# Rotary scores over 128 rows, SwiGLU blocks turned off TensorE, HGRN2 queries and forget features token-major

## The chip, the core and the metric

The kernel runs on one core of one Trainium2 chip. The metric is the time of one execution on the device in microseconds (us), lower is better. A core has TensorE (PE in the profile: matmuls, with the load of the stationary operand shown apart as PEld), VectorE (DVE), ScalarE (ACT), GpSimd (POOL) and the queue engine SyncE (SP), which issues most transfers here.

## What is computed

One layer on 256 tokens of width 2048, in float32: a half-step SwiGLU feed-forward (width 5632), a mixer of two branches (HGRN2, a gated linear recurrence over chunks of 64 tokens with 16 heads of 128, and latent attention with 16 heads whose scores have a 128-wide plain part and a 64-wide rotary part), a read of a memory of 256 rows, and a second SwiGLU half-step. Cut to what the change touches:

```python
def swiglu_half_step(x, pre_g, w_gate, w_up, w_down, post_g):
    h = rms_norm(x, pre_g)
    y = (jax.nn.silu(h @ w_gate) * (h @ w_up)) @ w_down
    return x + FFN_RESIDUAL_WEIGHT * rms_norm(y, post_g)
...
    q_full = jnp.concatenate([q_nope, q_pe], axis=-1)          # 128 + 64 per head
    k_full = jnp.concatenate(
        [k_nope, jnp.broadcast_to(k_pe[:, :, None, :], (B, S, MLA_HEADS, QK_ROPE))], axis=-1)
    o_b = chunk_causal_attention(q_full, k_full, v, MLA_QK ** -0.5)
...
    q_in = jax.nn.silu(q_hg.astype(f32)).reshape(B, S, HG_HEADS, HG_KDIM)
    o_a = hgrn2_chunk_scan(q_in, k_in, log_f, v_in).astype(x.dtype)   # k_in, log_f from f_hg
```

## The kernel before

Every large product is made of three matmuls: weights and activations are each split into a high part in the fp32r format and the rest (`whi`, `wlo`; `hh`, `hl`), and hi*hi + lo*hi + hi*lo are added up in PSUM. The small products of attention and HGRN2 are plain float32 matmuls, and the trace shows each of those as two records, called passes here. Weights stream from memory in pieces of 128x1024 (a "pair": two blocks of 128 rows by 512 columns), in the order of a list, `plan`. For each piece `feed` issues the transfer of `raw`, an ACT cast to `whi` and a DVE subtraction to `wlo`; there are three buffers for split pieces, so the cast of a piece waits until TensorE has finished with the piece three before it. `gemm` holds activations (128 tokens wide) stationary and streams 512 weight columns: 12 matmuls per pair, a result of two PSUM banks (`m` = 0, 1 for the two halves of the tokens) laid out token-major. `gemm_T` holds weights stationary and streams all 256 tokens: 24 matmuls per pair, and the result is feature-major, which is what the following step needs.

In `ffn`, each of 44 blocks (22 per SwiGLU, in segments of 12 and 10) is one `gemm` named `gu` of 8 pairs; then ACT takes the silu into `sg`, DVE multiplies into `h`, four TensorE transposes bring `h` to `pT` feature-major, and `part_split` makes `fh` (ACT) and `fl` (DVE), the stationary operands of the product `dn` that ends the segment.

In `attend`, a head's scores for the two halves of the queries are each two matmuls into one bank, the plain part over 128 rows and the rotary part over 64 rows (rows 0 to 63 or 64 to 127 by the head's parity, against `kpeT`, which holds the rotated key twice).

In `hgrn_units`, for each of four groups of four heads, the query `hq` and the forget feature `hf` are made by `gemm_T` (feature-major), the output gate `og` and the value `hv` by `gemm`, in the order hq, og, hv, hf. The query and forget features are scaled per token on DVE with `rB`, a broadcast of the norm factors. `hgrn` then runs a long chain of ACT and DVE steps (log, exp, a scan `b`, seven levels of exponentials `e`), with small matmuls `dg`, `lv`, `lx`, `o` between; all that overlaps the large products of the next group. PE, ACT and DVE each run their instructions in the order that the program's scheduler wrote them; an instruction that waits holds up those behind it on its engine.

Of the kernel before, what the change touches and what calls it, by code (L numbers as in the profile page):

```python
# [37 lines left out]
class Layer:  # L38
    def __init__(self, ctx, tc, A):
# [19 lines left out]
        self.q = []  # L59
        self.pending = []  # L60
        self.ident = self.cst.tile([P, P], F32, name="ident")
        make_identity(nc, self.ident)
# [22 lines left out]
    def feed(self, ahead):  # L85
        nc = self.nc
        while self.ready < min(self.at + ahead, len(self.plan)):
            src = self.plan[self.ready]
            spare = self.ready in self.spare
            n = src.shape[-1]  # L90
            raw = self.wraw.tile([P, n], F32, name=self.nm("raw"), tag="raw")
            nc.sync.dma_start(out=raw, in_=src)
            if spare:
                hi, lo = self.slot(self.spare[self.ready], "whi", F32R), self.slot(self.spare[self.ready], "wlo", F32R)
            else:
                hi = self.wsp.tile([P, n], F32R, name=self.nm("whi"), tag="whi")
                lo = self.wsp.tile([P, n], F32R, name=self.nm("wlo"), tag="wlo")
            nc.scalar.activation(hi, raw, AF.Copy)  # L98
            nc.vector.tensor_tensor(lo, raw, hi.bitcast(F32), ALU.subtract)  # L99
            self.q.append((hi, lo))  # L100
            self.ready += 1
# [9 lines left out]
    def gemm(self, act, k0, k1, name="g", head=0, tail=0, warm=0):  # L111
# [6 lines left out]
        for grp in groups:  # L118
            if grp[0] >= head and (grp[0] - head) % 2 == 0:
                self.settle(1)  # L120
            w = [self.weights(self.pending and grp[0] > head) for _ in grp]
            ks = [k0 + 2 * t + c for t in grp for c in range(2)]
            order = [(k, m) for k in ks for m in range(2)] if len(ks) == 2 else [(k, m) for m in range(2) for k in ks]
# [49 lines left out]
    def gain_split(self, hi, lo, pieces):  # L173
# [3 lines left out]
        for o, ps, g in pieces:  # L177
            self.last_lo = nc.vector.scalar_tensor_tensor(lo[:, o], ps, self.gc[:, g : g + 1], hi[:, o].bitcast(F32), ALU.mult, ALU.subtract)  # L178
        return ins

    def block_T(self, hi, lo, x, gcols=None, scale=None):
# [84 lines left out]
    def ffn(self, st, which, aside=None):  # L266
# [4 lines left out]
        for si, (b0, b1) in enumerate(SEG):  # L271
            quads = []
            for b in range(b0, b1):
# [9 lines left out]
                for m in range(2):  # L283
                    sg = self.tmp("sg")
                    nc.scalar.activation(sg[:, :256], ps[m][:, :256], AF.Silu, scale=r[m])
                    nc.vector.scalar_tensor_tensor(h[:, m * 256 : m * 256 + 256], ps[m][:, 256:], r[m], sg[:, :256], ALU.mult, ALU.mult)
                pt = self.bank("pT")
                for c in range(2):
                    for m in range(2):
                        nc.tensor.transpose(pt[:, c * 256 + m * P : c * 256 + m * P + P], h[:, m * 256 + c * P : m * 256 + c * P + P], self.ident)  # L290
                s = slice(512 * ((b - b0) % 2), 512 * ((b - b0) % 2) + 512)
                self.part_split(hi[:, s], lo[:, s], pt)
            fa = self.halves([q[0] for q in quads], [q[1] for q in quads])
# [73 lines left out]
    def mixer_consts(self):  # L367
        nc, v, c = self.nc, self.nc.vector, self.cst
        self.ones = c.tile([P, P], F32, name="ones")
        nc.gpsimd.memset(self.ones, 1.0)  # L370
        self.lmask = c.tile([P, 12 * 64], U8, name="lmask")
# [36 lines left out]
        nc.gpsimd.dma_start(out=fr, in_=self.A["invf"].to_broadcast([P, 32]))  # L408
        ang, n, tail, w = (c.tile([P, 64], F32, name=s) for s in ("ang", "angn", "angt", "angw"))
        for m_ in range(2):  # L410
# [68 lines left out]
    def key_pe(self, act, r):  # L479
# [22 lines left out]
        for m in range(2):  # L502
            nc.tensor.transpose(pt[:, m * P : m * P + P], k2[:, m * P : m * P + P], self.ident)
        self.kpeT = self.cst.tile([P, 256], F32, name="kpeT")
        nc.vector.tensor_copy(self.kpeT, pt[:, :256])

# [24 lines left out]
    def attend(self, g, qn, kn, qpe, value):  # L531
# [3 lines left out]
        for h in range(4):  # L535
            c = 256 * h
            rows = slice(64 * (h % 2), 64 * (h % 2) + 64)
            pc = 256 * ((4 * g + h) // 2 % 4)
            ps = self.bank("sc")
            for m, n0 in ((0, 0), (1, P)):  # L540
                w = P + P * m
                o = ps[:, n0 : n0 + w]
                nc.tensor.matmul(o, lhsT=qn[:, c + m * P : c + m * P + P], rhs=kn[:, c : c + w], start=True, stop=False)
                nc.tensor.matmul(o, lhsT=qpe[rows, pc + m * P : pc + m * P + P], rhs=self.kpeT[rows, :w], start=False, stop=True)
            s = self.tmp("s")
# [32 lines left out]

    def hgrn_units(self, g, act, actT, r, rB):
        nc = self.nc  # L580
        rb2 = rB.rearrange("p (o t) -> p o t", o=1).to_broadcast([P, 2, 256])


        def feature(ps, name, swap):
            o = self.slot("A", name)
            halves = lambda t: t.rearrange("p (h x t) -> p h x t", h=2, x=2)
            for i in range(2):
                ov, pv = halves(o[:, 512 * i : 512 * i + 512]), halves(ps[i])
                if not swap:
                    nc.vector.tensor_tensor(o[:, 512 * i : 512 * i + 512].rearrange("p (h t) -> p h t", h=2), ps[i].rearrange("p (h t) -> p h t", h=2), rb2, ALU.mult)  # L590
                    continue
                for x in range(2):
                    rx = rB[:, P * x : P * x + P].unsqueeze(1).to_broadcast([P, 2, P])
                    nc.vector.tensor_tensor(ov[:, :, 1 - x, :], pv[:, :, x, :], rx, ALU.mult)
            return o

        q = feature(self.gemm_T(actT, KC, "hq"), "q", True)
        nc.scalar.activation(q, q, AF.Silu)
        ps = self.gemm(act, 0, KC, "og")
        og = self.slot("A", "og")  # L600
        for m in range(2):
            nc.scalar.activation(og[:, m * 512 : m * 512 + 512], ps[m], AF.Silu, scale=r[m])
        ps = self.gemm(act, 0, KC, "hv")
        v = self.slot("A", "v")
        for m in range(2):
            nc.scalar.activation(v[:, m * 512 : m * 512 + 512], ps[m], AF.Identity, scale=r[m])
        f = feature(self.gemm_T(actT, KC, "hf"), "f", False)
        return q, f, v, og
# [137 lines left out]
    def mixer(self, st):  # L746
# [6 lines left out]
        for m in range(2):  # L753
            V.tensor_scalar(rh[:, m : m + 1], r[m], 0.5, None, ALU.mult)
        rB = self.cst.tile([P, 256], F32, name="rB")
        ps = self.bank("rB")
        for m in range(2):
            dg = self.tmp("dg")
            V.tensor_scalar(dg[:, :P], self.ident, r[m], None, ALU.mult)
            nc.tensor.matmul(ps[:, m * P : m * P + P], lhsT=self.ones, rhs=dg[:, :P], start=True, stop=True)  # L760
        V.tensor_copy(rB, ps[:, :256])
        qpe = [self.query_pe(self.gemm(self.halves(*cqT), 0, 4, "qr")) for _ in range(2)]
# [16 lines left out]
        for g in range(4):  # L779
            gr = self.hgrn_units(g, act, actT, r, rB)  # L780
            oa.append(self.hgrn(g, *gr))
# [26 lines left out]
    def plan_mixer(self):  # L808
# [7 lines left out]
        for j in range(4):  # L816
            pl += win(22 + j)
        group = lambda g: win(g) + win(12 + g) + win(8 + g) + win(4 + g)
        full = lambda k: [A[k][j, t] for j in range(4) for t in range(KC // 2)]
# [179 lines left out]
```

## Time and profile before

| | |
|---|---|
| median of 3 runs | 2651.07 us (2650.95 to 2651.12) |
| the profiled execution's own time | 2651.14 us |
| its span, first to last instruction | 2649.1 us, mean granted TensorE clock 0.999 |
| PE busy | 2622.8 us, 99% |
| DVE busy | 1497.3 us, 57% |
| ACT busy | 1311.8 us, 50% |
| transferred | 481.39 MB, mean 182 GB/s |

The profiled execution's time is its span and 2.0 us around it; it lies 0.07 us above the median. Busy time of PE counts a matmul from its start to its modelled end, and matmuls overlap: what one costs is read from start to start, not from its length.

### The profile page before, as it was taken

To read this page: it belongs to the slowest core of one execution; us is meant where nothing else is said; L and a number is where in the kernel's file an instruction comes from. 1 tells how busy PE (TensorE), PEld (TensorE's weight loads), DVE (VectorE), ACT (ScalarE), POOL (GpSimd) and SP (SyncE) were. 2 spreads that over 40 slices of the span, in tenths; PEclk is the share of its full clock that TensorE was granted. 3 is DMA by queue.
4 is the path that set the end of the run, shared out by engine and by line. 5 is a ranking of instruction groups with operands and counts; after the bars stand their busy time and mean duration, and the time that the engine had idled before them with its cause. 6 is when DMAs were issued, how large, how long until landed. Compare 5 with 4: busy or idle time off the path is not lost.

```text
span 2649.1 us, 33984 instructions
## 1 busy us (share of the span) xinstructions
PE 2622.8 (99%) x13136; PEld 2215.3 (84%) x13136; DVE 1497.3 (57%) x2004; ACT 1311.8 (50%) x1750; POOL 13.2 (0%) x36
## 2 busy tenths in 40 slices
PE   9999999999999999999999999999999999999998
PEld 7888888888888888889989988889788888888886
DVE  6555444554576544447577575657655554455555
ACT  5444444444455444346666664555644444444443
POOL 0000000000000000000000000000000000000000
PEclk9999999999999999999999999999999999999999
DMA  6655555555654346555545545665455556655564
GB/s 230 191 188 187 190 196 192 188 188 189 202 171 144 111 155 195 191 191 160 167 154 165 168 161 189 205 205 178 149 193 191 188 188 193 195 191 188 189 194 161
DMA packets 133714, 481.39 MB, mean 182 GB/s; under 512 B 15024, under 2 KB 15040, under 8 KB 133552
## 3 DMA queue, kind: packets, MB, share of 16 engines
q1 hardware_dynamic: 131472, 473.49, 55.4%
q0 software_dynamic: 1504, 4.68, 0.6%
q8 instruction: 103, 1.69, 0.3%
q10 hardware_dynamic: 576, 1.05, 0.1%
q14 instruction: 59, 0.48, 0.1%
HBM read 477.06 MB, written 2.10 MB: 181 GB/s over the span
## 4 chain that ended last, share of the span: by engine, by line
PE 96%; DVE 2%; DMA 1%; ACT 1%; issue 0%; SPq 0%; DVEq 0%; ACTq 0%
PE gu L130 12%; PE gu L129 12%; PE gu L128 12%; PE dn L128 6%; PE dn L129 6%; PE dn L130 6%; PE gate L130 2%; PE gate L128 2%; PE gate L129 2%; PE wo L129 1%; PE wo L130 1%; PE wo L128 1%; PE hf L352 1%; PE hf L351 1%; PE hf L350 1%; PE hv L129 1%
## 5 line engine op out<-in xcount | busy, mean ns | idle before, releaser
L99 DVE TENSOR_TENSOR wlo<-raw,whi 128x1024 fp32r<-128x1024 f32 x893 | 1092.5, 1225 | 1045.4 <-ACT whi L98 1044.3
L98 ACT ACTIVATE whi<-raw 128x1024 fp32r<-128x1024 f32 x893 | 945.9, 1060 | 1084.0 <-PE gu L130 444.9
L129 PE MATMUL gu<-wlo,hh 128*128 128x512 f32 x1408 | 552.1, 392 | 1.4 <-DVE wlo L99 1.4
L130 PE MATMUL gu<-whi,hl 128*128 128x512 f32 x1408 | 549.1, 390 | 0.7 <-DVE hl L178 0.7
L128 PE MATMUL gu<-whi,hh 128*128 128x512 f32 x1408 | 496.6, 393 | 1.8 <-ACT whi L98 1.5
L128 PEld LDWEIGHTS gu<-whi,hh 128*128 128x128 f32 x1408 | 263.9, 188 | 60.2 <-ACT whi L98 2.1
L130 PEld LDWEIGHTS gu<-whi,hl 128*128 128x128 f32 x1408 | 264.4, 188 | 55.7 <-DVE hl L178 1.5
L129 PEld LDWEIGHTS gu<-wlo,hh 128*128 128x128 f32 x1408 | 264.5, 188 | 55.0 <-DVE wlo L99 2.2
L129 PE MATMUL dn<-wlo,fh 128*128 128x512 f32 x704 | 274.2, 390 | 0.0
L130 PE MATMUL dn<-whi,fl 128*128 128x512 f32 x704 | 274.0, 389 | 0.0
L128 PE MATMUL dn<-whi,fh 128*128 128x512 f32 x704 | 247.1, 390 | 0.0
L128 PEld LDWEIGHTS dn<-whi,fh 128*128 128x128 f32 x704 | 132.1, 188 | 27.8
L130 PEld LDWEIGHTS dn<-whi,fl 128*128 128x128 f32 x704 | 132.2, 188 | 27.3
L129 PEld LDWEIGHTS dn<-wlo,fh 128*128 128x128 f32 x704 | 132.2, 188 | 27.1
L129 PE MATMUL gate<-wlo,hh 128*128 128x512 f32 x256 | 100.7, 394 | 0.0
L130 PE MATMUL gate<-whi,hl 128*128 128x512 f32 x256 | 100.1, 391 | 0.0
L128 PE MATMUL gate<-whi,hh 128*128 128x512 f32 x256 | 91.8, 391 | 0.0
L351 PE MATMUL hf<-hl,whi 128*128 128x256 f32 x256 | 72.5, 284 | 0.0
L351 PE MATMUL hq<-hl,whi 128*128 128x256 f32 x256 | 72.4, 284 | 0.0
L350 PE MATMUL hf<-hh,whi 128*128 128x256 f32 x256 | 72.3, 283 | 0.0
L350 PE MATMUL hq<-hh,whi 128*128 128x256 f32 x256 | 72.1, 283 | 0.0
L352 PE MATMUL hf<-hh,wlo 128*128 128x256 f32 x256 | 71.8, 283 | 0.0
(358 smaller groups left out, 3544.3 us busy)
## 6 DMA issues: line engine op xcount, KB each, us to landing
raw<-in_ffn_gu_dram SPq DMA_DIRECT2D x352, 512.0 KB, 3.4
raw<-in_win_dram SPq DMA_DIRECT2D x208, 512.0 KB, 3.5
raw<-in_ffn_dn_dram SPq DMA_DIRECT2D x176, 512.0 KB, 3.5
raw<-in_wbb_dram SPq DMA_DIRECT2D x32, 512.0 KB, 3.4
raw<-in_wba_dram SPq DMA_DIRECT2D x32, 512.0 KB, 3.5
raw<-in_wo_dram SPq DMA_DIRECT2D x32, 512.0 KB, 3.6
gb<-in_grow_dram POOLq DMA_DIRECT2D x16, 256.0 KB, 4.6
raw<-in_qup_n_dram SPq DMA_DIRECT2D x8, 512.0 KB, 3.4
```

What stands on the lines that cost most here:

```text
L98: nc.scalar.activation(hi, raw, AF.Copy)
L99: nc.vector.tensor_tensor(lo, raw, hi.bitcast(F32), ALU.subtract)
L128: nc.tensor.matmul(ps[m], lhsT=ah, rhs=wh[:, c], start=(k == k0), stop=False)
L129: nc.tensor.matmul(ps[m], lhsT=ah, rhs=wl[:, c], start=False, stop=False)
L130: self.last_mm = nc.tensor.matmul(ps[m], lhsT=al, rhs=wh[:, c], start=False, stop=(k == k1 - 1))
L350: nc.tensor.matmul(o, lhsT=wh[:, c], rhs=ah, start=first, stop=False)
L351: nc.tensor.matmul(o, lhsT=wh[:, c], rhs=al, start=False, stop=False)
L352: nc.tensor.matmul(o, lhsT=wl[:, c], rhs=ah, start=False, stop=last)
```

## The change

Four edits. (1) `ffn` no longer transposes `h` on TensorE: `turn` has DVE transpose `h` within blocks of 32x32 (`hb`), and 16 ACT copies of 32 partitions by 128 values put the blocks where the full transpose has them (`hT`); `part_split` reads `hT`. These ACT jobs are deferred: four strips to a job and the split as a fifth, one job behind each weight cast from the third pair after the block on. (2) `hq` and `hf` become `gemm` calls, token-major like `og` and `hv`; ACT scales them (with the silu, for the query) into `ta`, DVE transposes the 32x32 blocks into `tb`, and 16 strips for each half of the tokens, alternating between ACT and DVE, put them in place. The order of a group is now hq, og, hf, hv. (3) The rotary part of the scores contracts over all 128 rows, against a key tile `kpeT` that holds zeros in the other head's 64 rows. (4) `rB` and its two matmuls are gone.

```diff
@@ feed, gemm
-            nc.scalar.activation(hi, raw, AF.Copy)
+            self.last_hi = nc.scalar.activation(hi, raw, AF.Copy)
...
             w = [self.weights(self.pending and grp[0] > head) for _ in grp]
+            if self.later and self.later[0][0] <= self.at:
+                with self.tc.issue_after(self.last_hi.ins):
+                    self.later.pop(0)[1]()
@@ new
+    def turn(self, h, hi, lo):
+        nc = self.nc
+        b, o = self.tmp("hb"), self.tmp("hT")
+        nc.vector.transpose(b, h)
+        bv = b.rearrange("p (m c q t) -> p m c q t", m=2, c=2, q=4)
+        ov = o.rearrange("p (c m x t) -> p m c x t", c=2, m=2, x=4)
+        def strips(x):
+            for q in range(4):
+                nc.scalar.activation(ov[32 * q : 32 * q + 32, :, :, x, :], bv[32 * x : 32 * x + 32, :, :, q, :], AF.Copy)
+        self.defer([lambda x=x: strips(x) for x in range(4)] + [lambda: self.part_split(hi, lo, o)])
+    def defer(self, jobs):
+        self.later += [(self.at + 3, f) for f in jobs]
+    def turn_heads(self, ps, r, func, name, swap):
+        nc = self.nc
+        o = self.slot("A", name)
+        ov = o.rearrange("p (c m x t) -> p m c x t", c=4, m=2, x=4)
+        def strips(b, m, half):
+            bv = b.rearrange("p (c q t) -> p c q t", c=4, q=4)
+            for x in (2 * half, 2 * half + 1):
+                for q in range(4):
+                    to, src = ov[32 * q : 32 * q + 32, m, :, x, :], bv[32 * x : 32 * x + 32, :, q, :]
+                    if (x + q) % 2 == 0:
+                        nc.scalar.activation(to, src, AF.Copy)
+                    else:
+                        nc.vector.tensor_copy(to, src)
+        for m in range(2):
+            a, b = self.tmp("ta"), self.tmp("tb")
+            nc.scalar.activation(a, ps[m], func, scale=r[m])
+            nc.vector.transpose(b, a)
+            self.defer([lambda b=b, m=(1 - m if swap else m), x=x: strips(b, m, x) for x in range(2)])
+        return o
@@ ffn
-                pt = self.bank("pT")
-                for c in range(2):
-                    for m in range(2):
-                        nc.tensor.transpose(pt[:, c * 256 + m * P : c * 256 + m * P + P], h[:, m * 256 + c * P : m * 256 + c * P + P], self.ident)
...
-                self.part_split(hi[:, s], lo[:, s], pt)
+                self.turn(h, hi[:, s], lo[:, s])
@@ key_pe
-        self.kpeT = self.cst.tile([P, 256], F32, name="kpeT")
-        nc.vector.tensor_copy(self.kpeT, pt[:, :256])
+        self.kpeT = self.cst.tile([P, 512], F32, name="kpeT")
+        nc.gpsimd.memset(self.kpeT, 0.0)
+        for h in range(2):
+            nc.vector.tensor_copy(self.kpeT[64 * h : 64 * h + 64, 256 * h : 256 * h + 256], pt[64 * h : 64 * h + 64, :256])
@@ attend
-                nc.tensor.matmul(o, lhsT=qpe[rows, pc + m * P : pc + m * P + P], rhs=self.kpeT[rows, :w], start=False, stop=True)
+                nc.tensor.matmul(o, lhsT=qpe[:, pc + m * P : pc + m * P + P], rhs=self.kpeT[:, kc : kc + w], start=False, stop=True)
@@ hgrn_units
-        q = feature(self.gemm_T(actT, KC, "hq"), "q", True)
-        nc.scalar.activation(q, q, AF.Silu)
+        q = self.turn_heads(self.gemm(act, 0, KC, "hq"), r, AF.Silu, "q", True)
...
+        f = self.turn_heads(self.gemm(act, 0, KC, "hf"), r, AF.Identity, "f", False)
         ps = self.gemm(act, 0, KC, "hv")
...
-        f = feature(self.gemm_T(actT, KC, "hf"), "f", False)
```

In the order of ACT's instructions, one block of the first SwiGLU (the second `gu` product ends, the third runs) stood so before; `whi` are the casts of weight pieces:

```order
L98 ACTIVATE whi_680<-raw_678 128x1024
L285 ACTIVATE sg_645<-gu_498,ry_379 128x256
L98 ACTIVATE whi_698<-raw_696 128x1024
L285 ACTIVATE sg_648<-gu_499,ry_393 128x256
L98 ACTIVATE whi_716<-raw_714 128x1024
L98 ACTIVATE whi_734<-raw_732 128x1024
L169 ACTIVATE fh_404<-pT_651 128x512
```

The same stretch of a block on ACT in the changed kernel:

```order
L332 ACTIVATE sg_830<-gu_663,ry_379 128x256
L99 ACTIVATE whi_879<-raw_877 128x1024
L332 ACTIVATE sg_833<-gu_664,ry_393 128x256
L99 ACTIVATE whi_901<-raw_899 128x1024
L197 ACTIVATE hT_837<-hb_836 32x2x2x32 x8
L99 ACTIVATE whi_923<-raw_921 128x1024
L197 ACTIVATE hT_837<-hb_836 32x2x2x32 x4
L99 ACTIVATE whi_945<-raw_943 128x1024
L197 ACTIVATE hT_837<-hb_836 32x2x2x32 x4
L99 ACTIVATE whi_967<-raw_965 128x1024
L173 ACTIVATE fh_827<-hT_837 128x512
```

The split moves from behind four casts to behind six, and sixteen strips stand between the casts, eight of them in one run.

In the HGRN2 stage, on ACT around the end of a group's recurrence (`sx` is the copy of the small product `lx`, `sq` sums squares of the output `o`), the order before was:

```order
L98 ACTIVATE whi_10154<-raw_10152 128x1024
L715 ACTIVATE sx_9579<-lx_9581 128x512
L201 ACTIVATE sq_9594,sso_9589<-o_9587 128x128
L201 ACTIVATE sq_9596,sso_9589<-o_9587 128x128
L201 ACTIVATE sq_9598,sso_9589<-o_9587 128x128
L98 ACTIVATE whi_10172<-raw_10170 128x1024
```

In the changed kernel the query of the next group is taken out of PSUM there, with a load of an activation table ahead of it, and `whi_10234` is the cast of the fourth weight piece of `hf` (the tiles of pieces one to three are cast ahead of these rows):

```order
L99 ACTIVATE whi_10216<-raw_10214 128x1024
L743 ACTIVATE sx_9756<-lx_9758 128x512
L223 ACT_TABLE_LOAD
L223 ACTIVATE ta_9987<-hq_9840,ry_6139 128x512
...
L223 ACTIVATE ta_9991<-hq_9841,ry_6153 128x512
...
L217 ACTIVATE q_9986<-tb_9988 32x4x32 x5
L630 ACTIVATE og_10173<-og_9995,ry_6139 128x512
L630 ACTIVATE og_10173<-og_9996,ry_6153 128x512
L217 ACTIVATE q_9986<-tb_9992 32x4x32 x4
...
L99 ACTIVATE whi_10234<-raw_10232 128x1024
```

Between two casts there were four short instructions; now there are two `ta`, two `og`, sixteen strips, five `sq` and a table load.

On PE, the `hf` product of the same group began so before, with both result banks (10209, 10210) in turn and 24 matmuls to a weight piece:

```order
L350 MATMUL hf_10209<-hh_5556,whi_10213 128x256
L351 MATMUL hf_10209<-hl_5560,whi_10213 128x256
L350 MATMUL hf_10210<-hh_5556,whi_10213 128x256
L351 MATMUL hf_10210<-hl_5560,whi_10213 128x256
L352 MATMUL hf_10209<-hh_5556,wlo_10214 128x256
```

It begins so in the changed kernel, 15 matmuls to the one bank (10176) from three pieces (10180, 10198, 10216), and then 15 to the other (10177) from the same pieces:

```order
L752 MATMUL o_9765<-v_9601,sx_9756 128x128
L132 MATMUL hf_10176<-whi_10180,hh_5859 128x512
L133 MATMUL hf_10176<-wlo_10181,hh_5859 128x512
L134 MATMUL hf_10176<-whi_10180,hl_5863 128x512
...
L132 MATMUL hf_10176<-whi_10216,hh_5860 128x512
L133 MATMUL hf_10176<-wlo_10217,hh_5860 128x512
L134 MATMUL hf_10176<-whi_10216,hl_5864 128x512
L132 MATMUL hf_10177<-whi_10180,hh_5859 128x512
```

The bank 10177 is the one that `hq` held; the first piece is used up after 21 matmuls of 512 columns. The run of DVE's recurrence between two splits (a scan, two masked products, one product, four steps on f) is the same in both kernels; the split behind it belonged to the first piece of the next group's `og` before, and belongs to the fifth piece of its `hq` now.

## Rows read from the trace of the kernel before

**Rows 1.** The page, busy us by engine (share of the span), instructions.

```profile
PE 2622.8 (99%) x13136; PEld 2215.3 (84%) x13136; DVE 1497.3 (57%) x2004; ACT 1311.8 (50%) x1750; POOL 13.2 (0%) x36
```

**Rows 2.** The page, the chain that ended last, shares of the span by engine.

```profile
PE 96%; DVE 2%; DMA 1%; ACT 1%; issue 0%; SPq 0%; DVEq 0%; ACTq 0%
```

**Rows 3.** Windows: from:to length, busy (instructions) of PE PEld DVE ACT POOL, PEclk, DMA.

```profile
414.02:636.32 222.30, 222.30 (x998) 183.31 (x996) 112.21 (x107) 98.90 (x110) 0.00 (x0) 1.00 0.59 189
636.32:745.66 109.34, 109.34 (x485) 90.44 (x484) 61.99 (x69) 48.87 (x57) 1.61 (x3) 1.00 0.67 208
1024.39:1111.43 87.04, 87.04 (x385) 72.10 (x384) 43.01 (x39) 34.73 (x34) 0.00 (x0) 1.00 0.59 194
1111.43:1134.46 23.03, 23.03 (x193) 23.02 (x192) 11.28 (x12) 8.47 (x8) 0.00 (x0) 1.00 0.58 184
1134.46:1156.25 21.79, 21.79 (x98) 18.03 (x97) 10.77 (x11) 11.20 (x11) 0.00 (x0) 1.00 0.60 192
1201.04:1305.11 104.07, 103.04 (x694) 94.91 (x693) 73.45 (x114) 68.62 (x100) 0.00 (x0) 1.00 0.52 162
```

**Rows 4.** Timeline of PE, three transposes inside a gu product: start us, length us.

```profile
67.05 0.39 PE L128 MATMUL gu<-whi,hh 128*128 128x512 f32 x1
67.28 0.49 PE L290 MATMUL pT<-ident,h 128*128 128x128 f32 x3
...
67.84 0.40 PE L130 MATMUL gu<-whi,hl 128*128 128x512 f32 x1
68.08 0.40 PE L128 MATMUL gu<-whi,hh 128*128 128x512 f32 x1
```

**Rows 5.** Timeline of PE, scores of one group of four heads, first to last.

```profile
894.98 0.38 PE L543 MATMUL sc<-cp,cp 128*128 128x128 f32 x2
...
897.38 0.49 PE L544 MATMUL sc<-kpeT,qpeT 64*128 64x128 f32 x2
...
903.23 0.50 PE L128 MATMUL vv<-whi,ch 128*128 128x512 f32 x1
```

**Rows 6.** Tile sc, line 868 (memory read's scores, 128 rows): first and last start.

```profile
L868 PE MATMUL sc<-cp,cp x16: 377/379/379, 1848.8 to 1852.1; 128*128 128x256 f32 x16
```

**Rows 7.** The chain in order of time: start, us, piece; 128-column float32 passes.

```profile
1239.62 1.78 PE lv L684 x16
```

**Rows 8.** Groups of ACT by form, with mean ns of one behind the busy us.

```profile
L98 ACT ACTIVATE whi<-raw 128x1024 fp32r<-128x1024 f32 x893 | 945.9, 1060 | 1084.0 <-PE gu L130 444.9 <-PE dn L130 232.5 <-PE gate L130 56.7
L201 ACT ACTIVATE sq<-o 128x128 bf16<-128x128 f32 x32 | 8.8, 277 | 7.9 <-PE o L724 6.1 <-PE o L722 1.2
L732 ACT ACTIVATE on<-o,ry 128x128 f32<-128x128 f32 x32 | 8.6, 382 | 0.0
L201 ACT ACTIVATION_READ_ACCUMULATOR sq<-o 128x1 f32 x32 | 6.3, 195 | 0.0
L598 ACT ACT_TABLE_LOAD x4 | 5.1, 1283 | 0.1
L606 ACT ACTIVATE v<-hv,ry 128x512 f32<-128x512 f32 x8 | 5.8, 728 | 1.0 <-PE hv L130 1.0
```

**Rows 9.** Timeline of ACT: eight 128x128 activations back to back, start and length.

```profile
1279.66 2.16 ACT L732 ACTIVATE on<-o,ry 128x128 f32<-128x128 f32 x8
```

**Rows 10.** Groups of DVE by form, mean ns of one.

```profile
L99 DVE TENSOR_TENSOR wlo<-raw,whi 128x1024 fp32r<-128x1024 f32 x893 | 1092.5, 1225 | 1045.4 <-ACT whi L98 1044.3
L527 DVE COPY cp<-kn 128x512 f32<-128x512 f32 x8 | 5.5, 691 | 1.3 <-PE kn L352 1.2
L153 DVE SCALAR_TENSOR_TENSOR ry<-rt,ry 128x1 f32<-128x1 f32 x48 | 7.4, 157 | 0.8
```

**Rows 11.** Waits in 1201 to 1513 us: us in total, times, longest.

```profile
PE og L129 <- DVE wlo L99: 3.1, 3, 1.0
```

**Rows 12.** Timeline of DVE in one group: two wlo splits, first and last.

```profile
1218.40 1.23 DVE L99 TENSOR_TENSOR wlo<-raw,whi 128x1024 fp32r<-128x1024 f32 x1 [0.97 <-ACT whi L98]
...
1225.25 1.22 DVE L99 TENSOR_TENSOR wlo<-raw,whi 128x1024 fp32r<-128x1024 f32 x1
```

More of the change, by code (lines that the diff above doesn't have):

```diff
@@ L60, in __init__ @@
         self.pending = []
+        self.later = []
         self.ident = self.cst.tile([P, P], F32, name="ident")
@@ L368, in mixer_consts @@
         nc, v, c = self.nc, self.nc.vector, self.cst
-        self.ones = c.tile([P, P], F32, name="ones")
-        nc.gpsimd.memset(self.ones, 1.0)
         self.lmask = c.tile([P, 12 * 64], U8, name="lmask")
@@ L408, in mixer_consts @@
         nc.gpsimd.dma_start(out=fr, in_=self.A["invf"].to_broadcast([P, 32]))
-        ang, n, tail, w = (c.tile([P, 64], F32, name=s) for s in ("ang", "angn", "angt", "angw"))
+        wk = self.tmp("ang")
+        ang, n, tail, w = (wk[:, 64 * i : 64 * i + 64] for i in range(4))
         for m_ in range(2):
@@ L536, in attend @@
             c = 256 * h
-            rows = slice(64 * (h % 2), 64 * (h % 2) + 64)
+            kc = 256 * (h % 2)
             pc = 256 * ((4 * g + h) // 2 % 4)
@@ L576, in attend, with hgrn_units @@
         return hi, lo
-    def hgrn_units(self, g, act, actT, r, rB):
+    def hgrn_units(self, g, act, r):
         nc = self.nc
[L581 to L595, printed above, removed]
-        q = feature(self.gemm_T(actT, KC, "hq"), "q", True)
-        nc.scalar.activation(q, q, AF.Silu)
+        q = self.turn_heads(self.gemm(act, 0, KC, "hq"), r, AF.Silu, "q", True)
         ps = self.gemm(act, 0, KC, "og")
@@ L754, in mixer @@
             V.tensor_scalar(rh[:, m : m + 1], r[m], 0.5, None, ALU.mult)
[L755 to L761, printed above, removed]
         qpe = [self.query_pe(self.gemm(self.halves(*cqT), 0, 4, "qr")) for _ in range(2)]
@@ L779, in mixer @@
         for g in range(4):
-            gr = self.hgrn_units(g, act, actT, r, rB)
+            gr = self.hgrn_units(g, act, r)
             oa.append(self.hgrn(g, *gr))
@@ L817, in plan_mixer @@
             pl += win(22 + j)
-        group = lambda g: win(g) + win(12 + g) + win(8 + g) + win(4 + g)
+        group = lambda g: win(g) + win(12 + g) + win(4 + g) + win(8 + g)
         full = lambda k: [A[k][j, t] for j in range(4) for t in range(KC // 2)]
```

## The prediction

> **What bounds the kernel now.** The page comes first: TensorE is busy for 99% of the span, DVE for 57% and ACT for 50% [rows 1], and the chain of work that ended last lies on PE for 96% of the span [rows 2]. So a matmul taken away shortens the kernel by its own step, as long as DVE and ACT still deliver weights in time; work put on DVE or ACT costs nothing until a cast or a split of weights comes late. The windows give the prices by stage. Ten gu products of 96 matmuls fill 222.30 us, four bb products of the same 96 matmuls, with nothing between them, 87.04 us, which is 21.76 us a product and 0.2267 us a matmul of 512 columns; an hq product, 192 matmuls of 256 columns, takes 23.03 us, an og product right behind it 21.79 us [rows 3]. The granted clock is 1.00 in all of them, the 2.4 GHz level. In the gu window ACT is busy for 98.90 us and DVE for 112.21 us of 222.30 us [rows 3], so both have room there. One HGRN2 group takes 104.07 us, with DVE busy for 73.45 us [rows 3]; this is where PE waits.
>
> **SwiGLU transposes.** 44 blocks lose 4 transposes each, 176 in all. In the timeline three of them stand between two gu matmuls: from 67.05 to 68.08 us is 1.03 us, where three steps of 0.2267 us would take 0.68 us, so one costs 0.117 us and 176 cost 20.5 us [rows 4]. The windows give more: 222.30 - 10 x 21.76 = 4.7 us, and the dn window, which holds the transposes of the last block, is 109.34 us against 480 x 0.2267 = 108.8 us; together 5.2 us for ten blocks, 0.52 us a block, 23 us in all [rows 3]. I take 22 us, and keep 20.5 and 23.
>
> What replaces them must stay hidden. DVE gets one 32x32-block transpose of 128x512 a block. The trace has none; the nearest row of that size is a copy of 128x512 at 0.69 us [rows 10], and a two-times slower one would still fit, as DVE works 112.21/10.2 = 11 us a block of 21.8 us. ACT gets 16 strips of 32x128. The nearest rows are 128x128 activations: 0.277 us alone from PSUM and 0.382 us alone with a per-row scale [rows 8], and eight back to back in 2.16 us, so (2.16 - 0.38)/7 = 0.25 us a step [rows 9]. I take 0.25 us, with 0.38 us as the upper bound (the same instruction with nothing overlapped) and 0.16 us as the lower (the shortest instruction of a neighbouring engine [rows 10]). A block's ACT time goes from 98.90/10.2 = 9.7 us to 13.7 us (15.8 us at the upper bound), of 21.8 us. The tightest place is the run of eight strips between two casts: a cast may start when the piece three before is used up, and its split is wanted two pieces later, 2 x 2.72 = 5.44 us; cast and split take 1.06 + 1.23 us [rows 8, 10], so 3.1 us are free. Eight strips push the next cast back by 1.06 + 2.0 - 2.72 = 0.3 us (1.4 us at the upper bound). That is inside, so I price this edit's cover at nothing; it would begin to show at about 0.6 us a strip. The split `fh` of a segment's last block comes some five pieces into dn, which wants it in piece 10 or 12.
>
> **hq and hf token-major.** 192 steps of 256 columns become 96 of 512: 23.03 us become 21.77 us, for eight products 8 x 1.26 = 10.1 us [rows 3].
>
> **Scores.** A group of four heads takes 903.23 - 894.98 = 8.25 us, 2.06 us a head, where every second pair of passes is 64 rows high [rows 5]. The same float32 passes, all 128 rows high, step by 3.3/15 = 0.22 us at 256 columns [rows 6] and 1.78/16 = 0.11 us at 128 columns [rows 7]; a head has four of each, 1.31 us. So the passes on either side of a change of height cost about 0.1 us more than their columns. With none left, 0.75 us a head is saved, 12 us for 16. In the first two groups other matmuls stand between the passes and some of the changes are missing already, so I take 10.5 us, and keep 9 and 12. The softmax behind the scores then gets its input faster than DVE works it off; I allow 0.5 us of new waits.
>
> **rB.** Two float32 matmuls, four passes of 0.11 us [rows 7]: 0.4 us.
>
> **The HGRN2 stage.** Before: 2 x 23.03 + 2 x 21.79 us of products and 116 passes of 0.11 us (dg, lv, lx, o and transposes) make 102.5 us of the 104.07 us [rows 3, 7], so 1.5 us a group is waiting, in three groups; 1.0 us of it is og waiting for a split [rows 11] that stood behind DVE's long run: 5.6 us between two splits [rows 12]. After, by the changed order, three places a group can wait:
>
> First, hf's first 15 matmuls all go to one bank, because the other still holds hq until ACT has taken `ta`. So the first three pieces come free late, the first after 21 matmuls (4.8 us) and not 12. ACT's row behind `sx` is: table load 1.28, two `ta` of 512 columns, like the 0.73 us of a scaled hv bank, two `og` at the same, sixteen strips at 0.25 and five sums of squares at 0.28 and 0.2 us for their read-out [rows 8]; with some 0.6 us for `sx` that makes 1.3 + 1.5 + 1.4 + 4.0 + 2.3 + 0.6 = 11 us before the cast of piece four. From the end of `lx` PE has 2.7 us of small passes and 36 matmuls, 8.2 us: it wants that piece at 10.9 us. Cast and split end at some 12.5 us, so about 1.3 us of waiting (0 at the lower strip price, 3.4 at the upper).
>
> Second, f is ready a third of a product into hv, later against PE's place than hf's end was, because strips and casts alternate on ACT; the DVE run of 5.6 us then falls on the fifth piece of the next hq: I reckon 0.7 us of waiting (0 to 3). Third, DVE's strips of f beside the split of hv's fourth piece: 0.2 us (0 to 1). That is 2.2 us a group in place of 1.5 us, so 0.7 us more in three groups: 2 us.
>
> **Where the Trainium skill speaks against this change.** The eight strips in a row step by 0.25 us [rows 9]. The Trainium skill ("VectorE: DVE Perf Modes", section on the TRN2 errata) says that ScalarE pays a fixed latency per instruction from SBUF, 224 cycles beside its elements, and advises against small tiles; at its 1.2 GHz a strip would be 0.29 us, an estimate from that page, and the sum would be 2 us longer, at 2613 us; the trace has the shorter step.
>
> **Sum.** 22 + 10.1 + 10.5 + 0.4 = 43.0 us less, 0.5 + 2 = 2.5 us more: about 40 us less than the profiled execution's 2651.14 us, 2611 us. That execution is the median's time within 0.07 us, so no correction is made.
>
> **Rivals.** (a) The waits vanish: strips at the lower price, the old 1.5 us x 3 gone as well and no new ones: 2651.1 - 43 - 4.5 = 2604 us. For it: ACT loses table loads too, since the silu of hq and of og now stand together. Against it: 11 us of ACT work without a cast.
> (b) The HGRN2 waits grow: strips at 0.38 us give 3.4 + 3 + 1 us a group, 22 us in three groups in place of 4.5 us: 2651.1 - 43 + 18 = 2626 us, and 2618 us halfway. For it: DVE and ACT already make PE wait there [rows 11].
> (c) The rotary edit does nothing: if the long steps came from the operands and not from the height, the 10.5 us stay: 2622 us. Against it: [rows 6, 7] have float32 passes of the same columns without them.
> (d) ACT becomes the bound of the SwiGLU blocks and the kernel is slower: 9.7 us and 16 strips must exceed 22.2 us a block and what the other edits give back, 21/44 = 0.5 us, so from 0.81 us a strip on; at 0.9 us a block takes 24.1 us and the kernel 2651 + 44 x 1.9 - 21 = 2714 us. No row of this size is above 0.4 us [rows 8]. The Trainium skill ("VectorE: DVE Perf Modes", rules for kernel authors) says to do a 128x128 transpose on TensorE where the result may go to PSUM; by that rule this is the case that holds. The trace speaks against it here, as each TensorE transpose stands on the chain [rows 2, 4].
>
> **How the numbers follow.** Main case 0.51 (2606 to 2618 us), (a) 0.17, (b) 0.20, (c) 0.07, (d) 0.04, and 0.01 for no change. The predicted time is the main case's, 2611 us. The range leaves out (d), most of the upper half of (b), and the case beyond (a): 2603 to 2624 us. A measurement here tells 0.2%, 5 us, from no change. Faster has 0.95, the same 0.01, slower 0.04.
>
> **What would show it.** In the changed profile: no pT<-ident,h rows and gu windows of 21.8 us a product; hq and hf in 128x512 form at 21.8 us each; four heads' scores in 5.3 us; strips near 0.25 us a step. hf (fourth piece) and hq (fifth piece) waiting for a cast or a split about 1 us a time would show the HGRN2 reckoning right; gu rows waiting for whi or wlo throughout would make the prediction wrong, and so would a block transpose on DVE of several us.

## The result, and the profile after

The changed kernel takes 2616.19 us, the median of four runs (2613.66 to 2618.0), beside 2651.1 us before: a ratio of 0.9867, 95% interval 0.985 to 0.9884, 35 us faster. The forecast was 2611 us, with 2603 to 2624 us as the range. The profiled execution took 2618.0 us, with a span of 2616.0 us.

The busy row of the page, which answers to [rows 1], and the chain by engine, which answers to [rows 2]:

```profile
PE 2586.7 (99%) x12188; PEld 2164.5 (83%) x12188; DVE 1549.7 (59%) x2166; ACT 1548.1 (59%) x2582; POOL 13.5 (1%) x36
```

```profile
issue 71%; PE 27%; DVE 1%; DMA 0%; POOL 0%; ACT 0%; DVEq 0%; POOLq 0%; ACTq 0%
```

PE's share is what it was, and ACT has taken on 236 us. The 71% at "issue" (time in which the chain's engine waited for nothing that the profile shows) stand where PE's 96% stood; with PE at work for 99% of the span they tell of no new wait, so the waits are read from windows and timelines.

The windows answer to [rows 3], in this order: the gu and dn products of the first feed-forward part's second segment, the four bb products, and the three HGRN2 groups in which one group's products run beside the recurrence of the group before (each from the first matmul of hq to that of the next product hq or gate). Columns as there.

```profile
410.54:628.14 217.60, 217.60 (x962) 180.24 (x960) 117.79 (x116) 141.57 (x254) 0.00 (x0) 1.00 0.59 194
628.14:736.95 108.81, 108.81 (x482) 90.12 (x481) 62.68 (x70) 53.61 (x73) 1.61 (x3) 1.00 0.64 210
1003.94:1090.97 87.03, 87.03 (x385) 72.09 (x384) 43.02 (x39) 34.72 (x34) 0.00 (x0) 1.00 0.58 194
1178.02:1283.14 105.12, 103.17 (x501) 85.99 (x500) 80.28 (x145) 74.42 (x132) 0.00 (x0) 0.98 0.49 161
1283.14:1388.06 104.92, 103.08 (x502) 85.99 (x501) 80.03 (x144) 74.42 (x132) 0.00 (x0) 0.98 0.50 161
1388.06:1491.40 103.34, 101.50 (x501) 84.83 (x500) 80.03 (x144) 74.25 (x132) 0.00 (x0) 1.00 0.49 162
```

The gu products now take 21.76 us each, as bb does, and dn 108.81 us: 4.70 and 0.53 us less, the 5.2 us for ten blocks that the prediction read from the windows. The HGRN2 groups are the surprise. With 96 matmuls of 512 columns in place of 192 of 256, in two products, each should have lost 2.5 us; they took 104.07 us before and take 105.12, 104.92 and 103.34 us now. And the granted clock, 1.00 throughout before, is 0.98 in two of them.

Four heads' scores, timeline of PE, answering to [rows 5]:

```profile
880.76 0.38 PE L588 MATMUL sc<-cp,cp 128*128 128x128 f32 x2
880.98 0.39 PE L589 MATMUL sc<-kpeT,qpeT 128*128 128x128 f32 x2
...
885.81 0.58 PE L132 MATMUL vv<-whi,ch 128*128 128x512 f32 x1
```

That is 5.05 us for the 8.25 us of before; 5.3 us was forecast. The new operations, in the groups by form of DVE and ACT (mean ns behind the busy us), answering to [rows 8, 10]:

```profile
L191 DVE STREAM_TRANSPOSE hb<-h 128x512 f32<-128x512 f32 x44 | 31.3, 711 | 1.5
L219 DVE COPY q<-tb 32x128 f32<-32x128 f32 x64 | 14.0, 219 | 1.0
L197 ACT ACTIVATE hT<-hb 32x128 f32<-32x128 f32 x704 | 216.2, 307 | 9.1 <-DVE hb L191 0.2
L217 ACT ACTIVATE q<-tb 32x128 f32<-32x128 f32 x64 | 19.5, 305 | 0.8
```

The block transpose costs what the copy of that size did. A strip costs 0.31 us, not the 0.25 us taken, and strips don't overlap: four in a row take 1.25 us.

Where the three groups wait (waits of PE in 1178 to 1492 us, answering to [rows 11]):

```profile
PE hf L132 <- ACT whi L99: 3.8, 3, 1.3
PE hf L133 <- DVE wlo L100: 1.6, 3, 0.5
```

og's wait is gone and hf's is new, once a group. The timeline of PE at the first of them, in hf's fourth piece:

```profile
1242.46 0.39 PE L134 MATMUL hf<-whi,hl 128*128 128x512 f32 x1
1244.11 0.74 PE L132 MATMUL hf<-whi,hh 128*128 128x512 f32 x2 [1.25 <-ACT whi L99]
1245.37 0.79 PE L133 MATMUL hf<-wlo,hh 128*128 128x512 f32 x1 [0.53 <-DVE wlo L100]
1245.96 0.63 PE L134 MATMUL hf<-whi,hl 128*128 128x512 f32 x1
1246.38 0.63 PE L133 MATMUL hf<-wlo,hh 128*128 128x512 f32 x1
```

From start to start the step is 1.65 us where 0.23 us would do (1.42 us lost to the cast), then about 0.7 us are lost to its split: 2.1 us. Behind it the steps are 0.427 us long and not 0.227 us. Windows over the wait, over what follows it, and over the same place in the third group tell why:

```profile
1242.46:1245.30 2.84, 1.13 (x4) 0.30 (x2) 1.22 (x2) 2.81 (x8) 0.00 (x0) 1.00 0.00 0
1245.30:1248.71 3.41, 3.34 (x8) 2.67 (x9) 3.26 (x10) 1.53 (x5) 0.00 (x0) 0.50 0.64 189
1452.20:1456.00 3.80, 2.02 (x8) 1.03 (x8) 2.12 (x2) 3.73 (x12) 0.00 (x0) 1.00 0.00 0
19.90:23.31 3.41, 3.41 (x9) 2.55 (x9) 3.19 (x7) 3.41 (x8) 0.00 (x0) 0.50 0.48 156
```

Behind the wait PE works at a granted clock of 0.50, the 1.2 GHz level, in the first two groups and not in the third, after the same wait; that costs 1.7 us each time. The last row is a third such stretch, in the first gu product, behind a step of 2.0 us at 16.1 us (1.06 us before).

ACT's row ahead of that cast (timeline of ACT; sx belongs to the recurrence, ta is hq out of its PSUM bank, L217 are q's strips):

```profile
1231.76 0.58 ACT L743 ACTIVATE sx<-lx 128x512 f32<-128x512 f32 x1
1232.36 1.28 ACT L223 ACT_TABLE_LOAD   x1
1233.66 0.69 ACT L223 ACTIVATE ta<-hq,ry 128x512 f32<-128x512 f32 x1
...
1235.31 0.93 ACT L217 ACTIVATE q<-tb 32x128 f32<-32x128 f32 x3
...
1238.38 1.27 ACT L630 ACTIVATE og<-og,ry 128x512 f32<-128x512 f32 x2
...
1241.33 1.26 ACT L217 ACTIVATE q<-tb 32x128 f32<-32x128 f32 x4
...
1243.01 1.04 ACT L99 ACTIVATE whi<-raw 128x1024 fp32r<-128x1024 f32 x1
```

From sx to the cast are 11.25 us, where the prediction had reckoned 11, and ACT is busy throughout. That the two agree is partly luck: the sixteen strips take 5.0 us where 4.0 us were reckoned, and the rest takes 6.2 us where some 7 us were.

### The profile page after: what moved, and what is told of

It reads as the page before. It is cut to its first block, busy times and chain, and to the rows that moved or that the text cites. A ratio compares the mean times of both kernels' runs of the same rounds, so it can differ in the third digit from the quotient of the medians.

```text
span 2616.0 us, 33089 instructions
## 1 busy us (share of the span) xinstructions
PE 2586.7 (99%) x12188; PEld 2164.5 (83%) x12188; DVE 1549.7 (59%) x2166; ACT 1548.1 (59%) x2582; POOL 13.5 (1%) x36
## 4 chain that ended last, share of the span: by engine, by line
issue 71%; PE 27%; DVE 1%; DMA 0%; POOL 0%; ACT 0%; DVEq 0%; POOLq 0%; ACTq 0%
PE gu L134 6%; PE gu L133 6%; PE gu L132 6%; PE dn L132 3%; PE dn L133 3%; PE dn L134 3%; DMA gb<-in_grow_dram 0%; DVE y L377 0%; POOL gb L302 0%; DVE wlo L100 0%; DVE rt L153 0%; PE pT L233 0%; DVE yo L307 0%; DVE ry L157 0%; DVE hl L182 0%
## 5 line engine op out<-in xcount | busy, mean ns | idle before, releaser
L197 ACT ACTIVATE hT<-hb 32x128 f32<-32x128 f32 x704 | 216.2, 307 | 9.1 <-DVE hb L191 0.2
L332 ACT ACTIVATE sg<-gu,ry 128x256 f32<-128x256 f32 x88 | 41.0, 465 | 41.2 <-PE gu L134 41.1
L132 PEld LDWEIGHTS gate<-whi,hh 128*128 128x128 f32 x256 | 48.1, 188 | 10.0
L133 PEld LDWEIGHTS gate<-wlo,hh 128*128 128x128 f32 x256 | 48.1, 188 | 9.6
L134 PEld LDWEIGHTS gate<-whi,hl 128*128 128x128 f32 x256 | 48.1, 188 | 9.6
```

Of the source, the lines that this page charges most:

```text
L132: nc.tensor.matmul(ps[m], lhsT=ah, rhs=wh[:, c], start=(k == k0), stop=False)
L133: nc.tensor.matmul(ps[m], lhsT=ah, rhs=wl[:, c], start=False, stop=False)
L134: self.last_mm = nc.tensor.matmul(ps[m], lhsT=al, rhs=wh[:, c], start=False, stop=(k == k1 - 1))
L197: nc.scalar.activation(ov[32 * q : 32 * q + 32, :, :, x, :], bv[32 * x : 32 * x + 32, :, :, q, :], AF.Copy)
```

## The experiments

Times are medians, beside 2651 to 2652 us for the kernel before on the same chip; ratios are to that kernel. The kernel before took 2651.1 us beside the changed kernel, 2651.8 us beside the first four experiments below, 2651.2 us beside the strips repeated, the strips of q later and the wait filled, and 2650.8 us beside the two halves, so a difference from the changed kernel can be off by 0.7 us. Line numbers in the rows are those of each experiment's own code, a few lines off the changed kernel's.

**SwiGLU transposes back on TensorE.** The rest as changed.

```diff
-                self.turn(h, hi[:, s], lo[:, s])
+                pt = self.bank("pT")
+                for c in range(2):
+                    for m in range(2):
+                        nc.tensor.transpose(pt[:, c * 256 + m * P : c * 256 + m * P + P], h[:, m * 256 + c * P : m * 256 + c * P + P], self.ident)
+                self.part_split(hi[:, s], lo[:, s], pt)
```

> The changed kernel with the four TensorE transposes of each SwiGLU block put back; scores, hq and hf stay as changed. Theory (each TensorE transpose cost its place on PE, and the strips that replaced them were hidden): the 20.0 us that the two feed-forward parts lost between the two traces come back, 2616.2 + 20 = 2636 us (2634 to 2639, with the 22 us of the prediction at the upper end). Rival (the strips' load on ACT takes part of it away again in casts that come late): ACT without the strips gives more back than the transposes cost, and the time stays below 2632 us.

Measured: 2637.02 us (2636.41 to 2638.28, ratio 0.9946, 0.9933 to 0.9958). That is 20.8 us more than the changed kernel, as the theory has it. The Trainium skill ("VectorE: DVE Perf Modes", rules for kernel authors) sends a 128x128 transpose to TensorE where the result may go to PSUM; in this kernel, where PE is busy for 99% of the span, these 20.8 us speak against that rule.

**Rotary scores over 64 rows.**

```diff
+            rows = slice(64 * (h % 2), 64 * (h % 2) + 64)
...
-                nc.tensor.matmul(o, lhsT=qpe[:, pc + m * P : pc + m * P + P], rhs=self.kpeT[:, kc : kc + w], start=False, stop=True)
+                nc.tensor.matmul(o, lhsT=qpe[rows, pc + m * P : pc + m * P + P], rhs=self.kpeT[rows, kc : kc + w], start=False, stop=True)
```

> The changed kernel with the rotary scores taken over 64 of the 128 rows again, same columns, same number of passes. Theory (a pass beside a change of height steps about 0.1 us longer): four heads' scores go from 5.3 to about 8.2 us, and the time from 2616.2 to 2627 us (2625 to 2628). Rival (the long steps came from something else): 2616 us, no change.

Measured: 2627.17 us (2622.46 to 2628.63, ratio 0.9905, 0.9891 to 0.9918), 11.0 us more. The same columns in the same number of passes cost more at the other height, so the height it is, and the rival falls. From the first dn product of the second segment to the first hq product its trace takes 474.1 us and the changed kernel's 462.8 us, 11.3 us apart. One pair of passes of the plain part and the rotary pair behind it, here and then in the changed kernel (timelines of PE):

```profile
914.58 0.70 PE L589 MATMUL sc<-cp,cp 128*128 128x256 f32 x2
915.21 0.70 PE L590 MATMUL sc<-kpeT,qpeT 64*128 64x256 f32 x2
```

```profile
909.72 0.60 PE L588 MATMUL sc<-cp,cp 128*128 128x256 f32 x2
910.15 0.59 PE L589 MATMUL sc<-kpeT,qpeT 128*128 128x256 f32 x2
```

The plain pair has the same 128 rows in both kernels, and takes 0.63 us from start to start here and 0.43 us there. So the passes of full height pay as well, 0.1 us each, and the price is that of the change, not of 64 rows as such.

The lowest of its runs is the profiled one: its three HGRN2 groups take 103.56, 103.26 and 103.32 us at a granted clock of 1.00, with the same waits in hf. So the stretches at 0.50 come in some executions and not in others.

**hq and hf as before.** Feature-major products of 256 columns, rB and the old order of hv and hf put back (`hgrn_units`, `rB`, `ones` and `group` as in the kernel before).

```diff
-            gr = self.hgrn_units(g, act, r)
+            gr = self.hgrn_units(g, act, actT, r, rB)
...
-        group = lambda g: win(g) + win(12 + g) + win(4 + g) + win(8 + g)
+        group = lambda g: win(g) + win(12 + g) + win(8 + g) + win(4 + g)
```

> The changed kernel with hq and hf made feature-major in 192 steps of 256 columns as before, with the row factors rB and the old order of hv and hf. Theory (the 10.1 us that 96 steps of 512 columns save are given back in three of the four groups, by PE waiting in the fourth piece of hf and a lower granted clock behind that wait): the groups go back to 104.07 us from 105.12, 104.92 and 103.34 us, the first group from 87.05 to 89.61 us, and rB costs 0.4 us, together 1.8 us more: 2618 us (2615 to 2620). Rival (the edit is worth what its steps say, and the waits belong to the other edits): 2624 to 2626 us.

Measured: 2617.08 us (2616.62 to 2617.28, ratio 0.9869, 0.9856 to 0.9883). This edit, forecast to be worth 8.5 us (10.1 us and 0.4 us for rB, less 2 us of waits), is worth 0.9 us, inside the spread of the changed kernel's runs. Its three groups take 104.07, 104.08 and 104.08 us again, and og's wait is back:

```profile
PE og L133 <- DVE wlo L100: 3.1, 3, 1.0
```

**hq out of PSUM early.** ta and tb of hq come from the pool of the gain rows, which is idle here, instead of the ring of six buffers that scB, qx and sx use; ta is a plain scaling, and Silu follows on the finished q.

```diff
+            if swap:
+                a, b = (self.gb.tile([P, 512], F32, name=self.nm(t), tag="gb") for t in ("ta", "tb"))
+            else:
+                a, b = self.tmp("ta"), self.tmp("tb")
-            a, b = self.tmp("ta"), self.tmp("tb")
-            nc.scalar.activation(a, ps[m], func, scale=r[m])
+            nc.scalar.activation(a, ps[m], AF.Identity, scale=r[m])
...
+        if swap:
+            self.defer([lambda: nc.scalar.activation(o, o, func)])
```

> The changed kernel, but hq leaves its PSUM banks through two buffers of its own and by a plain scaling, so that ACT may take it while the recurrence still runs; the Silu of q follows once for all of q. Theory (hf's fourth piece waits because ACT's two evacuations of hq, sixteen strips and the sums of squares stand in one row behind the recurrence, ahead of its cast): the three waits of about 2.1 us and the lower clock behind two of them (1.7 us each) go, 2608 us (2606 to 2610), no step above 1 us in hf, and the granted clock stays at 1.00. Rival (q's strips and copies then stand between the recurrence's rows on ACT and DVE, and the wait moves to a split of og or to the recurrence's own passes): 2614 to 2620 us, with new waits in og.

Measured: 2609.86 us (2607.01 to 2611.41, ratio 0.9842, 0.9829 to 0.9855), 6.3 us less than the changed kernel. The windows of the three groups, the only wait in them, and ACT's row, where ta now stands 30 us earlier in its group, inside the recurrence:

```profile
1175.88:1278.08 102.20, 101.14 (x501) 84.83 (x500) 80.48 (x145) 75.69 (x134) 0.00 (x0) 1.00 0.50 167
1278.08:1379.92 101.84, 100.91 (x502) 84.83 (x501) 80.14 (x144) 75.43 (x133) 0.00 (x0) 1.00 0.50 165
1379.92:1481.82 101.90, 100.95 (x502) 84.84 (x501) 80.18 (x144) 75.49 (x133) 1.08 (x2) 1.00 0.53 170
```

```profile
PE og L133 <- DVE wlo L100: 2.8, 3, 0.9
```

```profile
1200.75 0.69 ACT L226 ACTIVATE ta<-hq,ry 128x512 f32<-128x512 f32 x1 [1.22 <-PE hq L134]
```

hf's wait and the low clock are gone, and the groups take 102.20, 101.84 and 101.90 us, as forecast for the change (102.1 us by the prediction's step). The rival was half right: og waits for its split again, 1.1 us from start to start, as in the kernel before.

**That edit's two halves.** First the scaling alone, then the buffers alone.

> The changed kernel with the plain scaling of hq (Silu of q once, afterwards) but without buffers of its own: ta and tb stay in the ring of six buffers in which the recurrence's scB, qx and sx come first. Theory (the ring, which is handed out in program order, puts ta behind sx): ACT still takes ta after sx, hf's fourth piece still waits for its cast about 2 us in three groups, and the time is that of the changed kernel, 2615 to 2618 us. Rival (the Silu's table load held ta back): the wait goes, 2608 to 2611 us.

Measured: 2614.63 us (2613.4 to 2615.9), a little under the theory's range and inside the spread of the changed kernel. The table load has moved, but ta has not (timeline of ACT):

```profile
1230.03 0.58 ACT L745 ACTIVATE sx<-lx 128x512 f32<-128x512 f32 x1
1230.51 0.68 ACT L223 ACTIVATE ta<-hq,ry 128x512 f32<-128x512 f32 x1
...
1235.20 1.28 ACT L632 ACT_TABLE_LOAD   x1
...
1241.14 1.04 ACT L99 ACTIVATE whi<-raw 128x1024 fp32r<-128x1024 f32 x1
```

> The changed kernel with hq's own two buffers but Silu still taken from PSUM. Theory (the ring alone held ta back): ta moves into the recurrence, hf's fourth piece no longer waits, and two table loads more in each of three groups, 1.28 us each on ACT between the recurrence's exponentials, come on top of og's wait of 1.1 us: 2609 to 2614 us. Rival (the buffers change nothing without the plain scaling): 2616 us with the wait in hf as it was.

Measured: 2609.74 us (2608.74 to 2610.37), with no wait in hf, og's wait as above, and six table loads more than the kernel with both halves, without a price that shows. So it is the ring of buffers, handed out in program order, that held ta behind sx; the plain scaling does nothing by itself.

**The wait filled.** The changed kernel, with PE kept at work through most of hf's wait by matmuls that add nothing (`zero` is a tile of zeros, `mixed` is set for the three groups beside a recurrence).

```diff
+            if name == "hf" and grp[0] == 3 and self.mixed:
+                with self.tc.issue_after(self.last_mm.ins):
+                    for _ in range(6):
+                        nc.tensor.matmul(ps[1][:, :P], lhsT=self.zero, rhs=self.ident, start=False, stop=False)
```

> The changed kernel with six float32 matmuls of 128 columns by a zero tile (12 passes, 1.3 us, adding nothing) ahead of hf's fourth piece in the three groups with a recurrence, so that PE works through most of its wait for the cast, which itself stays. Theory (the granted clock falls to 0.5 behind that idle time, and the 1.7 us of each fall are part of the 2616 us and of the spread of the runs): the clock stays at 1.00 in these groups, the fourth piece begins where it began, and the time is 2612.5 us (2611 to 2614), with a smaller spread. Rival (the falls have nothing to do with the idle time): rows of 0.5 remain, 2616 us or, if the passes do not fit into the wait, 2618 to 2620 us.

Measured: 2612.51 us (2611.52 to 2613.39, ratio 0.9854, 0.9839 to 0.9869). One of its windows and the timeline of PE at the wait:

```profile
1175.83:1279.17 103.34, 102.62 (x513) 86.41 (x512) 79.91 (x144) 74.36 (x132) 0.00 (x0) 1.00 0.49 162
```

```profile
1240.53 1.50 PE L132 MATMUL hf<-ident,zero 128*128 128x128 f32 x12
1241.96 0.73 PE L137 MATMUL hf<-whi,hh 128*128 128x512 f32 x2
```

The other two groups take 103.32 and 103.30 us, all at a clock of 1.00. The wait itself is as long as it was: a group without a low clock took 103.34 us before the filling. The three groups together are 3.4 us shorter than in the changed kernel's profile, which is two stretches at 1.7 us, and the mean granted clock is 0.999 in each of the four runs, where the changed kernel's runs have 0.996 to 0.998. One execution without low clock would prove little, as the scores over 64 rows had none either. But in the profiled executions of the six kernels that keep this wait (the changed one, and those with SwiGLU transposes on TensorE, scores over 64 rows, the scaling alone, and the strips twice and three times) 8 of the 18 groups have a stretch at 0.50; of the 15 groups of the five kernels without the wait (the one before, hq and hf as before, hq out of PSUM early, the buffers alone, q's strips later) none has. So the idle time brings the low clock; why behind one such wait and not behind another stays open.

**Strips twice and three times.** Each of the 16 ACT strips of a SwiGLU block is repeated.

```diff
-            for q in range(4):
+            for q in [0, 1, 2, 3] * 2:
```

> The changed kernel with each of the 16 ACT strips of a SwiGLU block done twice. Theory (the strips are covered as long as ACT needs less than a block's 21.76 us and the run of eight strips fits between two casts): ACT goes from 14.2 to 19.1 us a block, and a pair of strips, 0.62 us, lies at the 0.6 us from which the prediction let the run of eight begin to show: 0 to 1 us a block, 2616 to 2660 us. Rival (strips are not covered at all, each stands on the path): 44 x 4.9 us more, 2830 us.

Measured: 2694.29 us (2693.13 to 2694.97, ratio 1.0164, 1.0147 to 1.0181): 78 us more, 1.77 us a block, above the theory's 0 to 1 us. ACT is busy for only 18.5 us of a block's 23.3 us. The largest waits of PE, and ACT in one block:

```profile
PE gu L132 <- ACT whi L99: 24.7, 42, 1.5
PE gu L133 <- DVE wlo L100: 23.0, 43, 0.9
```

```profile
457.33 4.95 ACT L197 ACTIVATE hT<-hb 32x128 f32<-32x128 f32 x15
462.31 1.06 ACT L99 ACTIVATE whi<-raw 128x1024 fp32r<-128x1024 f32 x1
463.39 1.64 ACT L197 ACTIVATE hT<-hb 32x128 f32<-32x128 f32 x5
465.06 1.06 ACT L99 ACTIVATE whi<-raw 128x1024 fp32r<-128x1024 f32 x1
466.14 3.29 ACT L197 ACTIVATE hT<-hb 32x128 f32<-32x128 f32 x10
469.46 1.06 ACT L99 ACTIVATE whi<-raw 128x1024 fp32r<-128x1024 f32 x1
```

A cast that comes late is followed by more strips before the next, so the lateness adds up over three casts, and the third is the one that PE waits for (its matmul starts at 470.57 us).

> The changed kernel with each of the 16 ACT strips of a SwiGLU block done three times. Theory: ACT needs 14.2 + 9.8 = 24.0 us a block against 21.76 us and becomes the bound, 2.2 us a block more at least: 2713 us or more, slower than the kernel before, as the prediction's case of 0.81 us a strip and above has it. Rival (ACT and PE still overlap, because strips overlap each other or the order moves them): below 2660 us.

Measured: 2847.31 us (2846.33 to 2848.15, ratio 1.074, 1.0724 to 1.0756), 5.25 us a block above the changed kernel. The theory's bound held, but not its reason: ACT works 22.8 us of 26.5 us a block, so PE waits before ACT is full.

**Strips of q later.** The kernel with hq out of PSUM early, with q's strips put off to the end of og.

```diff
-            self.defer([lambda b=b, m=(1 - m if swap else m), x=x: strips(b, m, x) for x in range(2)])
+            self.defer([lambda b=b, m=(1 - m if swap else m), x=x: strips(b, m, x) for x in range(2)], 6 if swap else 3)
```

> The kernel with hq's own two buffers and plain scaling, with the strips of q put off by three pieces of weights more, to the end of og. Theory (the 1.1 us that og's fifth piece waits for its split in three groups come from q's strips and copies between the casts and splits): the waits go and the time is 2606.5 us (2605 to 2608). Rival (they come from the recurrence's own rows on ACT and DVE, as og waited 1.0 us in the kernel before too [rows 11]): 2609 to 2611 us.

Measured: 2609.97 us (2609.39 to 2610.72, ratio 0.9845, 0.983 to 0.986), with og's waits unchanged at 2.8 us in three. The rival holds: they are the recurrence's own, as before the change. My theory of og's wait falls.

The best version is thus hq out of PSUM early, 2609.9 us, or 2609.7 us with Silu left in place: 41 to 42 us below the kernel before, 6 us below the change.

## Why the prediction was right, and where its sizes were off

**SwiGLU transposes: right.** 22 us forecast, 20.8 us by the experiment. The profiled execution spent some 2 us more than most at the very start: 273.83 us for the first gu segment, beside 270.4 to 273.0 us in six experiments with the same blocks; the low-clock stretch there costs 1.7 us. The wait ahead of it is for the second piece of weights to land; PE is idle there for 1.75 us, for 0.5 us in two experiments and for 3.2 us in a third, which has such a stretch too (274.5 us), and it is no part of the edit. The second feed-forward part, up to its last dn product, went from 630.99 to 620.17 us, 10.8 us less, so some 22 us for two such parts. The cover held, but by less than reckoned. I had set the run of eight strips alone against 3.1 us of free time, and let it show from 0.6 us a strip; the strips between the later casts count too. With a strip doubled to 0.62 us the kernel is already slower than before, so case (d) begins below 0.62 us and not at 0.81 us: the measured 0.31 us is less far from it than I thought. Of the 4.9 us that doubling adds to a block 3.1 us were covered (4.9 - 1.77), which would put the onset near 0.5 us a strip if all beyond it showed; tripling adds 3.5 us a block for 4.9 us more of strips, and by that slope the onset is near 0.46 us. Both are estimates.

**The strip's price: mis-sized.** I took 0.25 us from 128x128 activations that read PSUM; it is 0.307 us from SBUF. The Trainium skill ("VectorE: DVE Perf Modes", the TRN2 errata) gave 0.29 us as an estimate; the trace agrees with it within 0.02 us, and the row that I preferred was of another source.

**Scores and rB: right.** 10.5 and 0.4 us less 0.5 us forecast; 11.0 us by the experiment for the scores. Case (c) is refuted by it.

**hq and hf: the products right, the waits too small.** The first group, with no recurrence beside it, went from 89.61 to 87.05 us, the 2.5 us forecast. The step that failed is "2.2 us a group in place of 1.5 us, so 0.7 us more in three groups: 2 us". By that step a group would have taken 102.1 us (four products of 21.76 us, 12.9 us of passes, 2.2 us). Without a low clock it takes 103.3 us, so 3.4 us are waited: 2.1 us in hf's fourth piece (1.3 forecast), and 1.3 us in many steps about 0.1 us too long, among which hq's fifth piece and hv's fourth, 0.9 us by the forecast, hardly stand out. In hf the row on ACT came out as reckoned, if partly by luck, and PE wanted the piece after 10.9 us, as forecast; but the cast and its split follow one another in full, 2.4 us, where my sum left 1.5 us for them. That is 3.6 us in three groups. The low clock, which no term held, adds 3.4 us in the profiled execution. Together 7 us; the forecast stayed in its range since this was its only large error. The other sizes were off by 1 us each and against one another, SwiGLU 1.2 us too high and the scores 1 us too low. The three experiments account for 20.8 + 11.0 + 0.9 = 32.7 of the 35 us; the rest is less than the 4.3 us by which the changed kernel's runs differ, and is given to no cause.

Case (b), waits that grow, is thus part of what happened: the three groups wait 5.7 us more than before the change where there is no low clock, a third of the 18 us of that case, and 9 us more in the profiled execution, half of it. I had read that ACT's row stands behind sx from the order of the instructions, without asking why; the ring of buffers is why, and it could be moved.

## What to carry to other kernels

Work that is hidden in an engine's idle time is priced by the deadlines of the casts between it, not by the engine's busy share: sum the lateness over all bursts up to the next free slot. An operand that leaves PSUM late may be held by a ring of temporary buffers handed out in program order, so look at who else uses the ring before blaming the engine. On a kernel bound by TensorE a wait has two prices, the wait and the clock behind it, and a saving of PE steps can turn into such a wait where the new operands pass through ACT and DVE ahead of the casts and splits that PE needs next.

## What the hardware showed unexpectedly

- Behind the wait in hf, 2.1 us lost to a cast and its split, the granted clock fell to 0.50 (1.2 GHz) in 8 of 18 groups over six profiled executions (two of three in the changed kernel, none with the scores over 64 rows), and in none of three when 1.5 us of that wait were filled with passes. The five kernels whose longest wait in these groups is 0.9 or 1.0 us [rows 11] showed no such stretch in 15 groups.
- A float32 pass beside a change between 128 and 64 rows steps by about 0.1 us more, whichever of the two it is itself: a plain pair of 256 columns took 0.63 us beside rotary passes of 64 rows and 0.43 us beside rotary passes of 128, 11.0 us over the kernel.
- Strips of 32x128 from SBUF on ACT take 0.31 us one after the other without overlap; DVE copies the same strip in 0.22 us, and its block transpose of 128x512 takes 0.71 us.
- Six extra table loads of 1.28 us, among the recurrence's exponentials on ACT, cost less than 1 us together: 2609.74 us with them and 2609.86 us without, where the kernel before took 2650.8 and 2651.8 us beside them.
